# Gate projections in pairs of output tiles: seven products of quarters in place of eight, with the sums on GpSimd

## The chip, the cores and the metric

The kernel runs on one core of one Trainium2 chip. The core has five engines that run side by side: TensorE (PE in the profile, PEld for its weight loads), VectorE (DVE), ScalarE (ACT), GpSimd (POOL) and SyncE (SP, which only starts DMA transfers here). Each takes its instructions in the order of its own queue and waits on semaphores. The metric is the device time of one execution in microseconds (us), lower is better. The kernel before has a median of 964.14 us over 3 runs (963.14 to 965.14).

## The reference

One layer of a mixer trunk in float32: 512 tokens of width 1024 pass a gated mixer of four branches, a cross-attention over 256 memory rows and a gated convolutional feed-forward block, each between RMS norms and with a residual. The part that the change touches is the mixer's gates:

```python
h = rms_norm(x, g[0])                       # (1, 512, 1024)
proj = h @ w_in                             # inputs of the four branches
ya, yb, yc, yd = shortconv(...), gla(...), sgu(...), rglru(...)    # each (1, 512, 256)
y_stack = jnp.stack([ya, yb, yc, yd], axis=2)
branch = jnp.einsum('bskc,kcd->bskd', y_stack, w_branch)           # 4 x 1024 outputs
gates = jax.nn.sigmoid((h @ w_gate).reshape(bsz, s, 4, 1024) + b_gate)   # w_gate: 1024 x 4096
merged = jnp.sum(gates * branch, axis=2)
return merged @ w_mix_out
```

After it follow `x + rms_norm(y)`, the attention, and the feed-forward block with `w_up` (1024 x 5632) and `w_down` (2816 x 1024).

## The kernel before, in words

All activations lie transposed: features on the 128 partitions, the 512 tokens along the free dimension. A projection makes one output tile of 128 features by 512 tokens in one PSUM bank. It runs over eight blocks of 128 input features, and for each block `mm3` (line 124) issues three matmuls, since every float32 operand is split into a high part that the fast float32 format of TensorE holds exactly and a low part that is the rest: high by high, high by low, low by high. So one output tile costs 24 matmuls of 512 columns with a 128x128 weight each.

A weight unit is 128 partitions by 1024 columns, the eight blocks of one output tile side by side (512 KB). `load_unit` (line 69) starts its DMA into a `raw` tile (ring of 4), ScalarE casts it to the high part `whi` (ring of 4, line 75), and VectorE subtracts to get the low part `wlo` (ring of 4, line 76). The list `plan` holds the units in the order of use; `unit` (line 101) loads `LOOK` = 2 units ahead of the one it gives out. A few units near the end (half of `w_o`, one of `w_up`, the last of `w_down`) go through `unit_kept` (line 106), which keeps the split parts in general slots of 512 columns.

The general slots are 76 tiles of 128 x 512 float32, handed out by `get` and returned by `put` (line 54). PSUM's eight banks are three groups: A with 2, B with 4, C with 2 (line 67). The program is written as a straight list of operations. The tile framework adds the semaphores and fixes, when the program is compiled, the order of each engine's queue; operations written earlier have priority, and `tc.high_priority()` raises a few.

Stages in order: load x and the first weights, with token sums of squares on the side (line 242 on); the 18 units of `w_in` (from line 581), between whose blocks `pump` advances the branch fibers (gated linear attention, recurrence, spatial gating), small generators of operations; the gate stage (line 631); the mixer's output projection (`mo`, line 692); keys and values of the memory, which have 256 columns (`kT`, line 729); attention; its output projection; the feed-forward block (`up`, `dn`); the output.

The gate stage runs over the four branches in the order 2, 3, 0, 1, and over eight output tiles each:

```python
    for ki, kb in enumerate(order):
        for m in range(KT):
            if m % 4 == 0:
                wb = unit()
            wg = unit()
            gp = bank("A", "gate")
            dense(gp, wg, xg)
```

`xg` are the eight split blocks of x times the norm's gain; the token's reciprocal norm `rb0s` is multiplied on afterwards, when VectorE drains the bank (`normed`, line 350, recorded at line 352). Then come the branch product of two blocks (six matmuls into a bank of group C), the sigmoid on ScalarE (line 643), gate times branch on VectorE (line 644) and the sum over the branches on VectorE (line 648). In the last branch the sum is split into parts (lines 651 and 152, 153) for the next projection. The original x stays in eight slots through the whole mixer, for the residual (line 707). The last fibers still run when the gate stage begins.

## Time and profile before

| | before |
|---|---|
| median of 3 runs | 964.14 us |
| profiled execution | 964.2 us, span 960.8 us |
| TensorE busy / instructions | 944.7 us (98%) / 4782 matmuls |
| VectorE busy | 575.4 us (60%) |
| ScalarE busy | 420.8 us (44%) |
| GpSimd busy | 11.9 us (1%) |
| DMA | 98.27 MB, mean 102 GB/s |

The span is the time from the first to the last instruction in the profile; the profiled execution's own time has a little around it. Matmuls are pipelined, so that a matmul's duration in the profile is longer than the distance to the next one, and "busy" of TensorE says only that it was not idle. A row of a group gives line, engine, operation, output and inputs, shapes and count, then busy time and mean duration in ns of one, then the engine's idle time just before these instructions with what ended it.

### The profile page before, as it was taken

How to read it: one execution, taken by the hardware profiler on the slowest of the kernel's cores; microseconds unless marked ns; L12 is line 12 of the kernel's file. 1: busy time of each engine (PE TensorE's matmuls, PEld its weight loads, DVE VectorE, ACT ScalarE, POOL GpSimd, SP SyncE). 2: the span in 40 equal slices, each digit the busy share in tenths (PEclk: the TensorE clock that was granted, in tenths of full speed). 3: DMA queues.
4: the chain of work that ended last, by engine and by line, in shares of the span. 5: the costliest groups of instructions: out<-in, count | busy, mean ns of one | idle time of the engine just before them, and what ended most of it. 6: DMA issues, size and time to landing. Idle time of an engine off the chain costs nothing.

```text
span 960.8 us, 12143 instructions
## 1 busy us (share of the span) xinstructions
PE 944.7 (98%) x4782; PEld 801.1 (83%) x4782; DVE 575.4 (60%) x886; ACT 420.8 (44%) x637; POOL 11.9 (1%) x33
## 2 busy tenths in 40 slices
PE   8999999999999999999999999999999999999996
PEld 8878887888888888899888899888888888888885
DVE  5876567535454567359854736887767777522414
ACT  7836336423232534356633645644444444322311
POOL 2000000000000000000000000000000000000001
PEclk9999999999999999999999999999999999999998
DMA  9432121232334332435322420232222323233302
GB/s 333 146 112 88 67 91 63 88 99 78 108 113 148 117 105 67 131 111 190 130 75 66 134 86 2 88 109 88 100 98 89 110 88 98 83 104 99 100 1 87
DMA packets 32648, 98.27 MB, mean 102 GB/s; under 512 B 4288, under 2 KB 7248, under 8 KB 32592
## 3 DMA queue, kind: packets, MB, share of 16 engines
q1 hardware_dynamic: 32416, 97.48, 31.2%
q8 instruction: 37, 0.61, 0.3%
q14 instruction: 19, 0.16, 0.0%
q0 software_dynamic: 32, 0.02, 0.0%
q10 hardware_dynamic: 144, 0.00, 0.0%
HBM read 95.39 MB, written 2.10 MB: 101 GB/s over the span
## 4 chain that ended last, share of the span: by engine, by line
PE 93%; DVE 2%; ACT 2%; issue 2%; DMA 0%; DVEq 0%; ACTq 0%
PE up L127 8%; PE up L126 8%; PE up L125 8%; PE gate L126 6%; PE gate L125 6%; PE gate L127 6%; PE dn L125 4%; PE dn L127 4%; PE dn L126 4%; PE win L125 3%; PE win L127 3%; PE win L126 3%; PE wo L125 2%; PE wo L127 2%; PE wo L126 2%
## 5 line engine op out<-in xcount | busy, mean ns | idle before, releaser
L75 ACT CAST whi<-raw 128x1024 fp32r<-128x1024 f32 x158 | 164.4, 1042 | 301.9 <-issue 142.0
L76 DVE TENSOR_TENSOR wlo<-raw,whi 128x1024 fp32r<-128x1024 f32 x158 | 191.3, 1213 | 130.1 <-ACT whi L75 128.8
L127 PE MATMUL up<-h3h,wlo 128*128 128x512 f32 (+1 forms) x368 | 138.2, 376 | 0.0
L126 PE MATMUL up<-h3l,whi 128*128 128x512 f32 (+1 forms) x368 | 138.1, 375 | 0.0
L125 PE MATMUL up<-h3h,whi 128*128 128x512 f32 (+1 forms) x368 | 138.1, 375 | 0.0
L125 PE MATMUL gate<-xgh,whi 128*128 128x512 f32 x256 | 99.8, 390 | 0.0
L126 PE MATMUL gate<-xgl,whi 128*128 128x512 f32 x256 | 99.7, 389 | 0.0
L127 PE MATMUL gate<-xgh,wlo 128*128 128x512 f32 x256 | 99.6, 389 | 0.0
L125 PEld LDWEIGHTS up<-h3h,whi 128*128 128x128 f32 x368 | 69.3, 188 | 12.6
L126 PEld LDWEIGHTS up<-h3l,whi 128*128 128x128 f32 x368 | 69.3, 188 | 12.4
L127 PEld LDWEIGHTS up<-h3h,wlo 128*128 128x128 f32 x368 | 69.3, 188 | 12.4
L352 DVE TENSOR_TENSOR sg<-gate,rb0s 128x512 f32<-128x512 f32 x32 | 22.1, 691 | 79.0 <-PE gate L127 78.9
L544 DVE SCALAR_TENSOR_TENSOR c<-u,par,c 128x511 f32<-128x511 f32 (+1 forms) x88 | 65.0, 746 | 1.3
L125 PE MATMUL dn<-gh,whi 128*128 128x512 f32 x154 | 59.9, 389 | 0.0
L126 PE MATMUL dn<-gl,whi 128*128 128x512 f32 x154 | 59.9, 389 | 0.0
L127 PE MATMUL dn<-gh,wlo 128*128 128x512 f32 x154 | 59.9, 389 | 0.0
L125 PE MATMUL win<-xgh,whi 128*128 128x512 f32 x144 | 57.1, 397 | 1.8 <-DVE la L535 1.8
L125 PEld LDWEIGHTS gate<-xgh,whi 128*128 128x128 f32 x256 | 48.1, 188 | 10.1
L126 PEld LDWEIGHTS gate<-xgl,whi 128*128 128x128 f32 x256 | 48.1, 188 | 9.9
L127 PE MATMUL win<-xgh,wlo 128*128 128x512 f32 x144 | 56.3, 391 | 0.0
L127 PEld LDWEIGHTS gate<-xgh,wlo 128*128 128x128 f32 x256 | 48.1, 188 | 9.9
L126 PE MATMUL win<-xgl,whi 128*128 128x512 f32 x144 | 56.1, 390 | 0.0
(348 smaller groups left out, 1729.9 us busy)
## 6 DMA issues: line engine op xcount, KB each, us to landing
raw<-in_w_up SPq DMA_DIRECT2D x44, 512.0 KB, 3.5
raw<-in_w_gate SPq DMA_DIRECT2D x32, 512.0 KB, 3.5
raw<-in_w_in SPq DMA_DIRECT2D x18, 512.0 KB, 3.6
raw<-in_w_down SPq DMA_DIRECT2D x16, 512.0 KB, 3.6
raw<-in_w_br SPq DMA_DIRECT2D x8, 512.0 KB, 3.4
raw<-in_w_mix SPq DMA_DIRECT2D x8, 512.0 KB, 3.5
raw<-in_w_k SPq DMA_DIRECT2D x8, 512.0 KB, 3.6
raw<-in_w_v SPq DMA_DIRECT2D x8, 512.0 KB, 3.5
```

Source lines behind the costliest of these rows:

```text
L75: scalar.copy(hi[:, :n], raw[:, :n])
L76: vector.tensor_tensor(lo[:, :n], raw[:, :n], hi[:, :n].bitcast(F32), op=ALU.subtract)
L125: tensor.matmul(ps, lhsT=w[0], rhs=x[0], start=first, stop=False)
L126: tensor.matmul(ps, lhsT=w[0], rhs=x[1], start=False, stop=False)
L127: tensor.matmul(ps, lhsT=w[1], rhs=x[0], start=False, stop=last)
L352: vector.tensor_tensor(t, ps, rb0s, op=ALU.mult)
L544: vector.scalar_tensor_tensor(dst[:, s:S], src[:, 0:S - s], pc(wname, (taps - 1 - s) * stride + off), dst[:, s:S], op0=ALU.mult, op1=ALU.add)
```

## The change

The gate projections take two output tiles at a time. The two weight tiles (256 outputs by 1024 inputs) are cut into quarters: A11 and A12 are the first tile's input blocks 0 to 3 and 4 to 7, A21 and A22 the second's. The input is cut into quarters too: blocks 0 to 3 and 4 to 7, tokens 0 to 255 and 256 to 511 (B11, B12, B21, B22). The four quarters of the result need eight products of quarters; the form of Strassen and Winograd needs seven, with sums of quarters made before and after:

- weights, on GpSimd for each pair: S1 = A21 + A22, S2 = S1 - A11, S3 = A11 - A21, S4 = A12 - S2
- tokens, once, before the later `w_in` units: T1 = B12 - B11, T2 = B22 - T1, T3 = B22 - B12, T4 = B21 - T2, on GpSimd, from copies of x times gain that VectorE makes; each is split into parts again
- products in the order A11 B11, S2 T2, A12 B21, S3 T3, S1 T1, A22 T4, S4 B22, each over four blocks with three matmuls of 256 columns. Three of them add onto an earlier product in the same half bank.

The sums after the products are made when a half bank is drained: one copy on ScalarE, the rest on VectorE, with two multiplications by `rb0s` from SBUF. Weight sums are split into high and low parts as the weights are. A pair makes splits of 1024, 1024, 512 and 1024 columns where two units made two of 1024.

Other edits come with it. The sum over branches is made on GpSimd. The `raw` ring has 5 tiles, `whi` and `wlo` have 6, two tiles `ws` hold the weight sums, the general slots are 70, and the framework's DMA scratch is set smaller. PSUM group A has 3 banks and B has 3. x is given back after the token sums and loaded again after the gate stage. The kept unit of `w_up` and those of `w_down` become ordinary units of the ring. The small load of `walpha` is started by SyncE and not by GpSimd.

```diff
-NSLOT = 76
+NSLOT = 70
+RAW, WHL = 5, 6
...
-        return pp.tile([P, S], F32, tag=tag, bufs={"A": 2, "B": 4, "C": 2}[tag], name=f"{name}_{serial[0]}")
+        return pp.tile([P, S], F32, tag=tag, bufs={"A": 3, "B": 3, "C": 2}[tag], name=f"{name}_{serial[0]}")
+
+    def split_w(src, n):
+        hi = wp.tile([P, 1024], F32R, tag="whi", bufs=WHL, name=f"whi_{serial[0]}")
+        lo = wp.tile([P, 1024], F32R, tag="wlo", bufs=WHL, name=f"wlo_{serial[0]}")
+        serial[0] += 1
+        scalar.copy(hi[:, :n], src)
+        vector.tensor_tensor(lo[:, :n], src, hi[:, :n].bitcast(F32), op=ALU.subtract)
+        return hi, lo
+
+    def load_pair(ap0, ap1):
+
+        raws = []
+        for ap in (ap0, ap1):
+            serial[0] += 1
+            raws.append(wp.tile([P, 1024], F32, tag="raw", bufs=RAW, name=f"raw_{serial[0]}"))
+            sync.dma_start(raws[-1], ap)
+        a11, a12, a21, a22 = [r[:, c:c + S] for r in raws for c in (0, S)]
+        wa, wb = [wp.tile([P, 1024], F32, tag="ws", bufs=2, name=f"ws{i}_{serial[0]}") for i in range(2)]
+        s2, s3, s4, s1 = wa[:, 0:S], wa[:, S:], wb[:, 0:S], wb[:, S:]
+        gpsimd.tensor_add(s1, a21, a22)
+        gpsimd.tensor_sub(s2, s1, a11)
+        gpsimd.tensor_sub(s3, a11, a21)
+        gpsimd.tensor_sub(s4, a12, s2)
+        h0, h1, h3, h2 = split_w(raws[0], 1024), split_w(wa, 1024), split_w(a22, S), split_w(wb, 1024)
+        at = {"a11": (h0, 0), "a12": (h0, S), "s2": (h1, 0), "s3": (h1, S), "a22": (h3, 0), "s4": (h2, 0),
+              "s1": (h2, S)}
...
-        for m in range(KT):
+        for m in range(0, KT, 2):
             plan += [(a["w_br"][kb * 2 + m // 4], 1024)] if m % 4 == 0 else []
-            plan += [(a["w_gate"][kb * KT + m], 1024)]
+            plan += [(a["w_gate"][kb * KT + m], a["w_gate"][kb * KT + m + 1])]
...
-    plan += [(a["w_up"][j], 1024) for j in js[:3]]
+    plan += [(a["w_up"][j], 1024) for j in js]
...
-    for m in range(KT - 1):
+    for m in range(KT):
         plan += [(a["w_down"][m][:, c0 * P:c1 * P], (c1 - c0) * P) for c0, c1 in pieces]
...
-    gpsimd.dma_start(walpha, a["w_alpha"])
+    sync.dma_start(walpha, a["w_alpha"])
...
+    def token_sums():
+
+        out = {n: [] for n in ("b11", "b21", "b22", "t1", "t2", "t3", "t4")}
+        for k in range(KT // 2):
+            x0, x1 = get("xs"), get("xs")
+            vector.tensor_scalar(x0, x[k], gn0[:, k:k + 1], None, op0=ALU.mult)
+            vector.tensor_scalar(x1, x[k + 4], gn0[:, k + 4:k + 5], None, op0=ALU.mult)
+            t12, t34 = get("t12"), get("t34")
+            gpsimd.tensor_sub(t12[:, LO], x0[:, HI], x0[:, LO])
+            gpsimd.tensor_sub(t12[:, HI], x1[:, HI], t12[:, LO])
+            gpsimd.tensor_sub(t34[:, LO], x1[:, HI], x0[:, HI])
+            gpsimd.tensor_sub(t34[:, HI], x1[:, LO], t12[:, HI])
+            put(x0, x1)
+            for names, t in ((("t1", "t2"), t12), (("t3", "t4"), t34)):
+                hi, lo = split(t, "xt", True)
...
+    def seven(wt, xt, name):
+
+        def product(ps, w, xn, more=False):
+            for k in range(4):
+                mm3(ps, wt(w, k), xt[xn][k], k == 0 and not more, k == 3, more)
+                if k % 2:
+                    pump()
+
+        def half():
+            return bank("A", name)[:, 0:256]
+
+        g0, g1, u = get(name), get(name), get("u23")
+        u2, u3 = u[:, LO], u[:, HI]
+        pa = half()
+        product(pa, "a11", "b11")
+        scalar.copy(u2, pa)
+        pb = half()
+        product(pb, "s2", "t2")
+        vector.tensor_tensor(u2, pb, u2, op=ALU.add)
+        product(pa, "a12", "b21", True)
+        vector.tensor_tensor(g0[:, LO], pa, rb0s[:, LO], op=ALU.mult)
+        pc_ = half()
+        product(pc_, "s3", "t3")
+        vector.tensor_tensor(u3, pc_, u2, op=ALU.add)
+        pd = half()
+        product(pd, "s1", "t1")
+        vector.tensor_tensor(g1[:, HI], pd, u3, op=ALU.add)
+        product(pc_, "a22", "t4", True)
+        vector.tensor_tensor(g1[:, LO], pc_, u2, op=ALU.add)
+        product(pd, "s4", "b22", True)
+        vector.tensor_tensor(g0[:, HI], pd, u2, op=ALU.add)
+        vector.tensor_mul(g1, g1, rb0s)
+        vector.tensor_mul(g0[:, HI], g0[:, HI], rb0s[:, HI])
+        put(u)
+        return g0, g1
...
     for p in R2:
         ps = w_in()
         vector.scalar_tensor_tensor(gl_q[p], ps, 0.125, gl_q[p], op0=ALU.mult, op1=ALU.mult)
+    xt = token_sums()
+    put(*x)
     for p in R2:
         rx = normed(w_in(), "rx")
...
-        for m in range(KT):
-            if m % 4 == 0:
+        for m0 in range(0, KT, 2):
+            if m0 % 4 == 0:
                 wb = unit()
-            wg = unit()
-            gp = bank("A", "gate")
-            dense(gp, wg, xg)
+            sgs = seven(unit(), xt, "gate")
             if kb == 1:
                 drain()
-            bp = bank("C", "br")
-            dense(bp, wb, y[kb], base=(m % 4) * 256)
-            sg = normed(gp, "sg")
-            scalar.activation(sg, sg, AF.Sigmoid, bias=pc("bgate", kb * KT + m))
-            vector.tensor_tensor(sg, bp, sg, op=ALU.mult)
-            if ki == 0:
-                acc[m] = sg
-            else:
-                vector.tensor_add(acc[m], acc[m], sg)
-                put(sg)
-                if ki == 3:
-                    merged.append(split(acc[m], "mg", True))
+            for m, sg in zip((m0, m0 + 1), sgs):
+                bp = bank("C", "br")
+                dense(bp, wb, y[kb], base=(m % 4) * 256)
+                scalar.activation(sg, sg, AF.Sigmoid, bias=pc("bgate", kb * KT + m))
+                vector.tensor_tensor(sg, bp, sg, op=ALU.mult)
+                if ki == 0:
+                    acc[m] = sg
+                else:
+                    gpsimd.tensor_add(acc[m], acc[m], sg)
+                    put(sg)
+                    if ki == 3:
+                        merged.append(split(acc[m], "mg", True))
...
+    x = [get(f"x{k}") for k in range(KT)]
+    for k in range(KT):
+        sync.dma_start(x[k], a["xT"][k])
...
-    kept = [unit_kept(a["w_down"][KT - 1][:, c0 * P:c1 * P], (c1 - c0) * P) for c0, c1 in pieces]
+    kept = [unit(0) for _ in pieces]
...
-    nc = _bacc.Bacc("TRN2", target_bir_lowering=False, num_devices=1)
+    nc = _bacc.Bacc("TRN2", target_bir_lowering=False, num_devices=1, dynamic_dma_scratch_size=1024)
```

56 lines of the change are left out of this document (33 added, 23 removed).

## The prediction

> **What bounds the kernel now.** I read the head of the page first, then the chain that ended last, then the stretches and groups of the gate stage, then single instructions.
>
> ```profile
> span 960.8 us, 12143 instructions
> PE 944.7 (98%) x4782; PEld 801.1 (83%) x4782; DVE 575.4 (60%) x886; ACT 420.8 (44%) x637; POOL 11.9 (1%) x33
> PE 93%; DVE 2%; ACT 2%; issue 2%; DMA 0%; DVEq 0%; ACTq 0%
> ```
>
> TensorE (PE) is busy in 98% of the span and holds 93% of the chain. VectorE (DVE) is at 60%, and GpSimd (POOL) is all but unused. The stretches show the same inside the gate stage, which begins near 149 us and ends near 374 us (columns: busy time and instructions of each engine, granted clock, DMA share):
>
> ```profile
> 75.00:149.00 74.00, 74.00 (x387) 61.31 (x386) 45.78 (x69) 33.79 (x42) 1.05 (x2) 1.00 0.26 86
> 149.20:163.00 13.80, 13.24 (x87) 10.60 (x85) 12.62 (x26) 7.70 (x11) 0.00 (x0) 1.00 0.11 39
> 204.21:258.80 54.59, 54.59 (x242) 45.25 (x241) 26.66 (x33) 15.47 (x19) 0.00 (x0) 1.00 0.31 97
> 373.30:418.00 44.70, 44.70 (x201) 37.07 (x200) 22.33 (x31) 21.43 (x31) 0.00 (x0) 1.00 0.33 106
> ```
>
> From 204 to 259 us, one branch's eight output tiles, PE never stops, at full clock (1.00). DVE is busy 26.66 of 54.59 us and ScalarE (ACT) 15.47, so only PE work counts there. At the beginning (149 to 163 us) it is otherwise: the last branch fibers keep DVE busy 12.62 of 13.80 us.
>
> A PE record's duration overlaps the next one's, so the price of a matmul is the distance between starts:
>
> ```profile
> 202.85 0.39 PE L125 MATMUL br<-ych,whi 128*128 128x512 f32 x1
> 209.65 0.39 PE L125 MATMUL br<-ych,whi 128*128 128x512 f32 x1
> 419.04 0.28 PE L126 MATMUL kT<-meml,whi 128*128 128x256 f32 x1
> 420.96 0.28 PE L127 MATMUL kT<-memh,wlo 128*128 128x256 f32 x1
> ```
>
> The first two rows are one output tile apart, 24 gate and 6 branch matmuls: 6.80 / 30 = 0.2267 us for 512 columns. The last two are 16 matmuls apart, each with a new 128x128 weight: 1.92 / 16 = 0.120 us for 256 columns. Half the columns cost 53% of the time. This is the form the change uses.
>
> **The change, part by part.**
>
> *PE.* A pair of output tiles now takes 2 x 8 x 3 = 48 matmuls of 512 columns, 48 x 0.2267 = 10.88 us. Afterwards it takes 7 products x 4 blocks x 3 = 84 of 256 columns, 84 x 0.120 = 10.08 us. The eighth less of arithmetic, 1.36 us, shrinks to 0.80. Sixteen pairs give 12.8 us. The twelve branch matmuls, 2.72 us, stay, so a pair's period on PE goes from 13.60 to 12.80 us. That is the whole possible gain, provided the other engines keep this pace.
>
> *DVE.* The rows that price it:
>
> ```profile
> L76 DVE TENSOR_TENSOR wlo<-raw,whi 128x1024 fp32r<-128x1024 f32 x151 | 184.6, 1225 | 108.3 <-ACT whi L75 107.0
> L352 DVE TENSOR_TENSOR sg<-gate,rb0s 128x512 f32<-128x512 f32 x32 | 22.1, 691 | 79.0 <-PE gate L127 78.9
> L644 DVE TENSOR_TENSOR sg<-br,sg 128x512 f32<-128x512 f32 x32 | 21.9, 685 | 4.0 <-ACT sg L643 4.0
> L648 DVE TENSOR_TENSOR sg<-sg,sg 128x512 f32<-128x512 f32 x24 | 16.6, 690 | 0.7
> L735 DVE TENSOR_TENSOR kl<-kT,kh 128x256 fp32r<-128x256 f32 x8 | 3.3, 417 | 0.3
> L786 DVE TENSOR_SCALAR p<-p,mx 128x256 f32<-128x256 f32 x16 | 4.9, 351 | 0.3
> ```
>
> Per pair before: two and a half weight splits (half a w_br unit), 3.06; normalisation 1.38, product with the branch 1.37, accumulation 1.38: 7.19 us. After: splits of 1024, 1024, 1024 and 512 columns and half a unit, 3 x 1.225 + 0.69 + 0.61 = 4.98; six drains of a half bank at 0.417, 2.50; two normalisations from SBUF, 0.69 + 0.42 = 1.11; the branch products 1.37. That is 9.96 us of 12.80, or 78%. The accumulations go to POOL.
>
> *ACT.*
>
> ```profile
> L75 ACT CAST whi<-raw 128x1024 fp32r<-128x1024 f32 x151 | 158.5, 1051 | 277.7 <-issue 142.0 <-PE win L126 31.1 <-PE dn L126 28.7
> L643 ACT ACTIVATE sg<-sg,par 128x512 f32<-128x512 f32 x32 | 23.0, 719 | 0.0
> L734 ACT CAST kh<-kT 128x256 fp32r<-128x256 f32 x8 | 2.9, 368 | 0.0
> ```
>
> Casts 3 x 1.05 + 0.63 + 0.53, two sigmoids 1.44 and the copy of the first half bank 0.37: 6.1 us of 12.80. Hidden behind PE. If a cast of 1.05 us stood just ahead of that copy, PE would wait 1.05 + 0.37 less the 1.44 us of the product between (12 x 0.120): nothing.
>
> *POOL.* It does four 512-column sums per pair and, from the second branch on, two accumulations. The trace has no such addition, only four of 256 columns at the very end, beside DVE:
>
> ```profile
> 953.49 0.72 POOL L978 TENSOR_TENSOR out<-x,out 128x256 f32<-128x256 f32 x1 [868.68 <-DVE out L976]
> 953.93 0.56 DVE L978 TENSOR_TENSOR out<-x,out 128x256 f32<-128x256 f32 x1
> 954.17 0.91 POOL L978 TENSOR_TENSOR out<-x,out 128x256 f32<-128x256 f32 x1
> 955.41 0.63 DVE L978 TENSOR_TENSOR out<-x,out 128x256 f32<-128x256 f32 x1
> L978 DVE TENSOR_TENSOR out<-x,out x12: 409/416/629, 945.0 to 957.0; 128x256 f32<-128x256 f32 x12
> L976 DVE TENSOR_TENSOR out<-rb,yg x16: 406/414/425, 944.4 to 956.3; 128x256 f32<-128x256 f32 x16
> 1.61 0.29 POOL masks.py:199 TENSOR_SCALAR_AFFINE_SELECT ident<-ident 128x128 f32<-128x128 f32 x1
> 27.94 0.63 POOL L315 TENSOR_SCALAR_AFFINE_SELECT sguw<-sguw 128x512 f32<-128x512 f32 x1 [10.69 <-DMA sguw<-in_sgu_wT]
> ```
>
> The last two rows give POOL's fixed part: 0.34 us for 384 columns leaves 0.18 us. An undisturbed 256-column addition is 0.72, so 0.54 scales, and 512 columns make 0.18 + 1.08 = 1.26 us. Bounds: 0.72 + 0.27, if it grew only as DVE does from 256 to 512 columns (0.417 to 0.69), to 2 x 0.91. I take 1.26, an estimate: 5.0 us per pair in the first branch, 7.6 after, of 12.80.
>
> *POOL against DVE.* The rows show a turn taken. The DVE addition that starts at 953.93, inside a POOL addition, takes 0.56 us, the one at 955.41 0.63, against 0.41 when alone; the POOL addition that follows takes 0.91 against 0.72. DVE's product of a PSUM operand and one SBUF tensor (L976) is not stretched, at most 0.425. So a DVE instruction with two SBUF operands and a POOL addition exclude each other. Not over their whole length: POOL's ended at 954.21, DVE's at 954.49, so 0.28 of its 0.41 us were exclusive. Per pair DVE has 4.98 + 1.11 = 6.09 us of that kind, in 6.5 instructions, some 4.2 exclusive (0.28/0.41); POOL's 7.6 fit beside that, 11.8 of 12.80.
>
> [...]
>
> *What PE waits for.* Three half banks are used twice within a pair. Before its second use DVE or ACT must have drained the first result, in the 1.44 us of the product between. For the third bank (u3) and the fourth (g1, later tokens) the drain is DVE's. It stands in DVE's queue behind any split just started; behind it, in turn, stand the other drains and the splits of the next pair. Best: no stall. Worst: a 1.225 us split held by one POOL addition, then the drain: 1.26 + 1.225 + 0.42 - 1.44 = 1.47 us per pair, 23 us in all. I take 0.2 us, 3.2 in all, near the low end: a weight's slot comes free after the third product of a pair at the earliest (4.3 us), for a weight needed after the twelve branch matmuls (12.8), so splits have some 8 us to go and few must fall into these two windows; nearest row, L352, shows DVE waiting for PE in that place (79.0 us), not PE for DVE.
>
> *The first pair.* Its 9.96 us of DVE work meet a DVE with 13.80 - 12.62 = 1.2 us to spare. Between 0, if the drains go ahead of the fibers, and 8.8 us; I take 2.5, since weight splits of this pair can go earlier, where DVE idles 28 of 74 us.
>
> *Token sums and moves, once.*
>
> ```profile
> L152 ACT CAST mgh<-sg 128x512 fp32r<-128x512 f32 x8 | 5.0, 621 | 13.2 <-DVE sg L648 13.2
> L153 DVE TENSOR_TENSOR mgl<-sg,mgh 128x512 fp32r<-128x512 f32 x8 | 5.5, 692 | 4.7 <-ACT mgh L152 4.7
> L114 ACT CAST kwh<-raw 128x512 fp32r<-128x512 f32 x15 | 9.0, 633 | 4.3 <-DMA raw<-in_w_o 3.5 <-DMA raw<-in_w_up 0.5 <-DMA raw<-in_w_down 0.4
> L115 DVE TENSOR_TENSOR kwl<-raw,kwh 128x512 fp32r<-128x512 f32 x15 | 9.7, 686 | 1.6 <-ACT kwh L114 1.6
> raw<-in_w_mix SPq DMA_DIRECT2D x8, 512.0 KB, 3.5
> ```
>
> Eight scalings on DVE (at most 2 x 0.351 each) and eight splits (0.62 ACT, 0.69 DVE) are 11.1 us of DVE, sixteen POOL subtractions at 0.72 are 11.5 us, all in the 74 us before the gate stage, of which DVE idles 28. With the cover gone they delay the fibers that the first pair waits for: 0 to 3 us, I take 0.5. x is freed and loaded again, eight DMAs of 256 KB in SP's queue among weight loads, at a DMA share of 0.33. They equal four weight loads, 4 x 3.5 = 14 us if one followed the other; the two weights loaded ahead cover 48 x 0.2267 = 10.9. Nothing, or some 3 us if a weight queues behind all eight. Four kept weights become ring units, which saves two halves against a whole on both engines, 4 x (2 x 0.686 + 2 x 0.633 - 1.225 - 1.051) = 1.4 us if nothing hid it; PE shows no idle time there, so nothing. Nor do walpha's DMA, from POOL's queue to SP's, and a bank from group B to A change anything that PE waits for.
>
> *Sum.* The profiled execution took 964.2 us (span 960.8 and 3.4 around it), the median of the three runs is 964.14, so the sum can go against either. 964.2 - 12.8 + 3.2 + 2.5 + 0.5 = 957.6 us. By itself, with the small bounds of its terms: 952 to 962.
>
> **Rivals.**
>
> 1. All of the gain: drains and fibers never late, 964.2 - 12.8 = 951.4 us. For it: the rings' slack; DVE at 78%. Against: DVE at 91% where the stage begins.
>
> 2. No change: DVE and POOL exclude each other for whole instructions. A pair then needs 6.09 + 7.6 = 13.7 us in the last three branches, and PE's 12.80 in the first (6.09 + 5.0 is less). 12 x 13.7 + 4 x 12.80 = 215.6 against 16 x 13.60 = 217.6, that is -2.0, and with 2.5 + 0.5 from above 965.2 us. [...] Against: only 0.28 of 0.41 us exclusive.
>
> 3. Slower: DVE becomes the bound, as it stands idle in its queue while POOL adds. Each of the 6.5 two-SBUF instructions of a pair that waits half a POOL addition, 0.63 us, makes 9.96 + 4.1 = 14.06 us, 0.46 above the old period, in twelve pairs; the first branch has a third less of POOL and stays at PE's pace. 964.2 + 12 x 0.46 - 4 x 0.80 + 2.5 + 0.5 = 969.5 us. It decides from a wait of 0.44 us on (2.84 / 6.5), and loses against before from 0.56. A whole addition at each would end near 1020. For it: waits of 0.15 and 0.22 us in the only two meetings, with additions half as long. Against: the POOL sums come in one burst per pair, and then DVE is free of them.
>
> **How the numbers follow.** Forecast 0.45, rival 1 0.18, rival 2 0.14, rival 3 0.23. Predicted is the forecast's 957.6. Down, the range goes past the full gain with the 1.4 us of the kept weights, to 948. Up, it takes in rival 2 and the nearer half of rival 3, to 976. A measurement of this kernel tells about 0.2% (1.9 us) from no change. Faster by more: the forecast and rival 1, less a sliver, 0.62; within: 0.14; slower: 0.24.
>
> **What would show it.** Right: the 256-column matmuls of the stage start 0.120 us apart; a branch's eight tiles take 51 to 53 us in place of 54.6; PE's idle time in the stage is a few us, put down to DVE drains of half banks and most of it in the first pair; POOL additions of 512 columns take near 1.26 us, longer only beside DVE's two-SBUF instructions. Wrong: starts 0.13 us apart or more, since 0.1295 x 84 = 10.88 eats all of the gain; DVE over 95% busy in the stage; weight splits that wait for POOL and PE waiting for them; POOL additions of 1.6 us and more.

## The result, and the profile after

The changed kernel has a median of 985.72 us (984.65 to 986.06), against 964.21 us of the kernel before on the same chip: a ratio of 1.0222, with a 95% interval of 1.0204 to 1.0239. It is slower, by 21.5 us, where 957.6 had been forecast; the time lies above the whole range. Its profiled execution took 985.39 us.

The head of the changed kernel's page, and the chain that ended last:

```profile
span 983.6 us, 13661 instructions
PE 946.0 (96%) x5358; PEld 825.0 (84%) x5358; DVE 661.2 (67%) x1002; ACT 456.6 (46%) x688; POOL 161.6 (16%) x136
PE 81%; DVE 7%; issue 4%; ACT 3%; POOL 2%; DMA 2%; SPq 0%; DVEq 0%; ACTq 0%; POOLq 0%
```

The span grew by 22.8 us. TensorE holds 81% of the chain in place of 93%, and VectorE 7% in place of 2%. VectorE's 67% alone would not worry anyone: the average hides the stage that counts.

The span splits in three. The gate stage began at 149.4 us before and ended at 374.6, where the first `mo` matmul starts; now it begins at 157.2 and ends at 395.2. The kernel before, in stretches (busy time and instructions of PE, PEld, DVE, ACT, POOL; granted clock, DMA share, GB/s):

```profile
149.40:374.60 225.20, 224.64 (x1026) 185.91 (x1024) 121.05 (x163) 80.56 (x104) 0.00 (x0) 1.00 0.31 101
```

The changed kernel, the same view; the last five rows are short stretches behind stalls:

```profile
157.20:395.20 238.00, 221.41 (x1597) 208.20 (x1596) 189.65 (x263) 107.62 (x145) 120.61 (x78) 0.97 0.31 102
256.00:260.00 4.00, 4.00 (x22) 4.00 (x23) 1.69 (x4) 1.27 (x2) 0.58 (x1) 0.57 0.40 131
285.30:290.00 4.70, 4.70 (x26) 4.60 (x27) 3.08 (x5) 2.34 (x3) 1.28 (x2) 0.66 0.33 112
314.50:319.00 4.50, 4.46 (x31) 4.20 (x32) 3.08 (x6) 2.60 (x3) 1.10 (x2) 1.00 0.31 117
343.00:348.00 5.00, 5.00 (x33) 4.66 (x34) 3.63 (x6) 2.72 (x3) 1.58 (x2) 1.00 0.35 105
369.80:376.00 6.20, 6.20 (x30) 6.20 (x31) 3.48 (x6) 2.28 (x3) 1.92 (x2) 0.53 0.65 218
```

So 7.8 us were lost before the gate stage, 12.8 in it (238.0 against 225.2), and 2.2 behind it (588.4 us from there to the end of the span, against 586.2). Since the matmuls of the stage should have become 12.8 us shorter, the stage lost 25.6 us to something. TensorE is idle for 238.00 - 221.41 = 16.6 us of it, where it had been idle for 0.6: 16.0 more. Three stretches at a clock of 0.57, 0.66 and 0.53 cost, by estimate, (1 - clock) times their length, 1.7 + 1.6 + 2.9 = 6.2 us. Some 3.4 us are left over; the first experiment shows where most of them lie. The idle time is put down to these waits (engine, line, what it waited for: us in all, times, longest):

```profile
PE gate L159 <- DVE u L664: 10.2, 9, 1.8
PE gate L159 <- ACT u L656: 3.5, 2, 3.1
PE gate L159 <- DVE u L659: 2.4, 2, 1.4
```

Line 664 is the drain `u3`, line 659 the drain that makes `u2`, line 656 ScalarE's copy of the first half bank. No wait for a weight is among them. Here is the costliest kind, on the three engines in turn, as single instructions (start, duration; in brackets the idle time before it and what ended it):

```profile
251.42 1.28 POOL L91 TENSOR_TENSOR ws<-raw,ws 128x512 f32<-128x512 f32 x1
...
251.82 1.95 DVE L75 TENSOR_TENSOR wlo<-ws,whi 128x1024 fp32r<-128x1024 f32 x1 [0.62 <-ACT whi L74]
...
252.66 2.24 POOL L745 TENSOR_TENSOR gate<-gate,gate 128x512 f32<-128x512 f32 x1
...
253.69 0.40 PE L160 MATMUL br<-ydl,whi 128*128 128x512 f32 x1
253.70 1.75 DVE L75 TENSOR_TENSOR wlo<-raw,whi 128x512 fp32r<-128x512 f32 x1
...
255.38 0.41 DVE L664 TENSOR_TENSOR u<-gate,u 128x256 f32<-128x256 f32 x1
255.84 0.38 PE L159 MATMUL gate<-xth,whi 128*128 128x256 f32 x1 [1.75 <-DVE u L664]
```

Read it as two engines that pass one thing back and forth. POOL's L91 ends at 251.42 + 1.28 = 252.70. The split that started at 251.82 ends at 253.77, 1.07 us after that; alone it takes 1.22. The POOL addition that started at 252.66 ends at 254.90, 1.13 us after the split; alone it takes 1.28. The next split, 0.68 alone, started at 253.70 and ends at 255.45, 0.55 us after that addition. Each waits for the whole of the other and then runs nearly its full length; only some 0.15 us of its beginning lies beside the other. The drain `u3`, which waits in VectorE's queue behind the two splits, comes at 255.38, and TensorE has stood for 1.75 us.

The longest single wait, 3.08 us before 369.78 in the last branch, comes another way. There GpSimd does a branch sum (line 745) only after two weight sums that stand before it in its queue, and ends it at 368.81. ScalarE's cast of that sum (line 186) waits 4.14 us for it, and the copy of the first half bank (line 656), for which TensorE waits, stands behind the cast in ScalarE's queue. In the whole stage these casts wait:

```profile
ACT mgh L186 <- POOL gate L745: 10.5, 5, 4.1
```

With the low clock behind it (2.9 us) this one stall costs some 6 us.

Line 664 itself isn't stretched. The stage's groups in the changed kernel, by shape (count | busy us, mean ns | idle time before):

```profile
L745 POOL TENSOR_TENSOR gate<-gate,gate 128x512 f32<-128x512 f32 x22 | 32.4, 1485 | 12.0 <-DVE gate L741 12.0
L90 POOL TENSOR_TENSOR ws<-raw,raw 128x512 f32<-128x512 f32 x14 | 26.3, 1876 | 0.0
...
L109 DVE TENSOR_TENSOR wlo<-raw,whi 128x1024 fp32r<-128x1024 f32 x11 | 21.1, 1914 | 1.4 <-ACT whi L108 1.4
...
L75 DVE TENSOR_TENSOR wlo<-raw,whi 128x512 fp32r<-128x512 f32 x15 | 15.6, 1038 | 0.9 <-ACT whi L74 0.9
...
L664 DVE TENSOR_TENSOR u<-gate,u 128x256 f32<-128x256 f32 x16 | 6.6, 413 | 0.0
```

The 1914 ns of line 109 are a mixture: the seven `w_br` splits take 2.29 to 2.31 us each, and four splits of the next projection, at the end of the stage, 1.22 to 1.23. Splits of 512 columns take 1038 ns in the mean, POOL's additions up to 1876. The drains, with one operand in PSUM, keep their 413 ns.

### The profile page after: what moved, and what is told of

It is laid out like the page before. It is cut to its first block, busy times and chain, and to the rows that moved or that the text cites. A ratio compares the mean times of both kernels' runs of the same rounds, so it can differ in the third digit from the quotient of the medians.

```text
span 983.6 us, 13661 instructions
## 1 busy us (share of the span) xinstructions
PE 946.0 (96%) x5358; PEld 825.0 (84%) x5358; DVE 661.2 (67%) x1002; ACT 456.6 (46%) x688; POOL 161.6 (16%) x136
## 4 chain that ended last, share of the span: by engine, by line
PE 81%; DVE 7%; issue 4%; ACT 3%; POOL 2%; DMA 2%; SPq 0%; DVEq 0%; ACTq 0%; POOLq 0%
PE up L160 8%; PE up L161 8%; PE up L159 8%; PE dn L159 4%; PE dn L161 4%; PE dn L160 4%; PE gate L159 4%; PE gate L160 4%; PE gate L161 4%; PE win L159 3%; PE win L160 3%; PE win L161 3%; DVE wlo L75 2%; PE wo L159 2%; PE wo L161 2%
## 5 line engine op out<-in xcount | busy, mean ns | idle before, releaser
L109 DVE TENSOR_TENSOR wlo<-raw,whi 128x1024 fp32r<-128x1024 f32 (+1 forms) x130 | 164.9, 1273 | 126.2 <-ACT whi L108 124.6
L108 ACT CAST whi<-raw 128x1024 fp32r<-128x1024 f32 (+1 forms) x130 | 134.3, 1037 | 175.9 <-PE dn L160 62.8
L159 PE MATMUL gate<-xth,whi 128*128 128x256 f32 x256 | 75.2, 294 | 12.6 <-DVE u L664 10.2
L161 PE MATMUL gate<-xth,wlo 128*128 128x256 f32 x256 | 73.6, 287 | 0.0
L160 PE MATMUL gate<-xtl,whi 128*128 128x256 f32 x256 | 73.5, 287 | 0.0
L161 PE MATMUL dn<-gh,wlo 128*128 128x512 f32 (+1 forms) x198 | 72.6, 367 | 0.0
L159 PE MATMUL dn<-gh,whi 128*128 128x512 f32 (+1 forms) x198 | 72.5, 366 | 0.0
L160 PE MATMUL dn<-gl,whi 128*128 128x512 f32 (+1 forms) x198 | 72.4, 366 | 0.0
L159 PEld LDWEIGHTS gate<-xth,whi 128*128 128x128 f32 x256 | 50.1, 196 | 16.8 <-DVE u L664 14.0
L159 PE MATMUL gate<-xgh,whi 128*128 128x256 f32 x192 | 56.3, 293 | 3.6 <-ACT u L656 3.5
```

Source lines behind the costliest of these rows:

```text
L108: scalar.copy(hi[:, :n], raw[:, :n])
L109: vector.tensor_tensor(lo[:, :n], raw[:, :n], hi[:, :n].bitcast(F32), op=ALU.subtract)
L159: tensor.matmul(ps, lhsT=w[0], rhs=x[0], start=first, stop=False, skip_group_check=more)
L160: tensor.matmul(ps, lhsT=w[0], rhs=x[1], start=False, stop=False, skip_group_check=more)
L161: tensor.matmul(ps, lhsT=w[1], rhs=x[0], start=False, stop=last, skip_group_check=more)
```

## The experiments

**Theory and rivals after the result.** Theory A: a POOL addition and a VectorE instruction with two SBUF operands exclude each other from end to end, so VectorE stands in its queue with the drains behind it, and that is what TensorE waits for. Theory B: VectorE simply has too much to do, or it is the order of the seven products. Theory C: the smaller rings and the other buffers. Beside these, the token sums were suspected of the 7.8 us at the beginning.

### GpSimd out of the gate stage

```diff
-        wa, wb = [wp.tile([P, 1024], F32, tag="ws", bufs=2, name=f"ws{i}_{serial[0]}") for i in range(2)]
-        s2, s3, s4, s1 = wa[:, 0:S], wa[:, S:], wb[:, 0:S], wb[:, S:]
-        gpsimd.tensor_add(s1, a21, a22)
-        gpsimd.tensor_sub(s2, s1, a11)
-        gpsimd.tensor_sub(s3, a11, a21)
-        gpsimd.tensor_sub(s4, a12, s2)
+        wa, wb = raws[1], raws[0]
...
-                    gpsimd.tensor_add(acc[m], acc[m], sg)
+                    vector.tensor_add(acc[m], acc[m], sg)
```

The weight sums are left out here: the products take raw quarters in their place, so the gates are not those of the reference. Splits, products, drains and token sums all stay.

> The changed kernel with GpSimd taken out of the gate stage: the four weight sums are left out (the raw quarters are split in their place, as many splits of the same size), and the sum over the branches is made on VectorE again. The products are then not those of the gates. Theory (VectorE's two-operand instructions and GpSimd's additions shut each other out, and that makes the drains late): TensorE's idle time in the stage falls under 6 us, splits are back at 1.22 us, the stage takes 215 to 223 us, the total is 963 to 971. Rival (VectorE is simply too full, and one product too short a time for a drain, whatever GpSimd does): idle time stays over 10 us, stage over 230, total over 977.

Measured: 960.05 us, ratio 0.9967 (0.9954 to 0.998). The gate stage as one stretch, then the only wait of PE in it, then two groups:

```profile
157.20:372.40 215.20, 214.00 (x1599) 202.56 (x1598) 175.99 (x287) 108.37 (x145) 0.00 (x0) 1.00 0.35 114
```

```profile
PE gate L154 <- DVE u L654: 1.0, 1, 1.0
```

```profile
L104 DVE TENSOR_TENSOR wlo<-raw,whi 128x1024 fp32r<-128x1024 f32 x11 | 13.4, 1220 | 1.4 <-ACT whi L103 1.4
...
L75 DVE TENSOR_TENSOR wlo<-raw,whi 128x512 fp32r<-128x512 f32 x15 | 10.3, 684 | 0.0
```

All of these splits are back at 1220 and 684 ns, where 2.31 us and 1038 ns stood. VectorE has more instructions than in the changed kernel (287 against 263), since the branch sums are its own again, and is busy for less time (175.99 against 189.65 us). The stage takes 215.2 us: 22.8 less than with POOL at work, and 10.0 less than before. So GpSimd's work in the stage cost 22.8 us. Theory A explains the splits and the drains behind them; the run also takes away the late branch sums of the last branch, and does not separate the two. Of theory B the part that says "too much to do" falls, at least for this amount of work.

By the prediction's sum the stage should take 225.2 - 12.8 = 212.4 us, and 2.8 us of the gain are still missing here, without any work on GpSimd. TensorE is idle for 1.2 us, and the pairs are 12.9 and 13.0 us apart in place of 12.80 (ScalarE's copies, line 651, start at 256.98, 269.86 and 282.86). So most of the 3.4 us that were left over above are no matter of late drains.

### The branch sums alone back on VectorE

```diff
-                    gpsimd.tensor_add(acc[m], acc[m], sg)
+                    vector.tensor_add(acc[m], acc[m], sg)
```

> The changed kernel with one edit: the sum over the branches is made on VectorE again; GpSimd keeps the weight sums. Theory (time in which GpSimd holds the shared operands): 24 of 88 additions, some 31 of 138 us of GpSimd's, are gone from the stage; TensorE's idle time falls from 16 to 6 to 11 us, the stage takes 224 to 232 us in place of 238, total 972 to 980 us. Rival (only the weight sums, which come in one burst per pair, meet the splits, and VectorE gets 17 us more to do): stage 236 us or more, total 983 or more.

Measured: 974.15 us, ratio 1.0102 (1.008 to 1.0124). The gate stage:

```profile
157.20:385.20 228.00, 217.98 (x1596) 204.17 (x1595) 201.75 (x286) 107.34 (x145) 88.17 (x56) 0.99 0.33 108
```

The stage is some 10 us shorter than the changed kernel's although VectorE does the additions now (the stretches of these runs begin up to 0.2 us off the first gate matmul). From 238.0 to 228.0 us here, and from there to the 215.2 of the run above: taken away in this order, the branch sums on POOL cost some 10 us, the weight sums on POOL another 13. In the first part is the stall of some 6 us in the last branch: the wait at line 656 falls from 3.5 to 0.5 us.

### Half as long, twice as many

Weight sums of 256 columns in place of 512, twice as many: if it is the longest single hold that matters, this helps; if the total time held, it harms.

```diff
-        gpsimd.tensor_add(s1, a21, a22)
-        gpsimd.tensor_sub(s2, s1, a11)
-        gpsimd.tensor_sub(s3, a11, a21)
-        gpsimd.tensor_sub(s4, a12, s2)
+        for q in (slice(0, 256), slice(256, S)):
+            gpsimd.tensor_add(s1[:, q], a21[:, q], a22[:, q])
+            gpsimd.tensor_sub(s2[:, q], s1[:, q], a11[:, q])
+            gpsimd.tensor_sub(s3[:, q], a11[:, q], a21[:, q])
+            gpsimd.tensor_sub(s4[:, q], a12[:, q], s2[:, q])
```

> The changed kernel with one edit: each weight sum on GpSimd is made in two instructions of 256 columns. Theory A (the length of one hold counts, since a drain waits behind a split that waits for one addition): a split waits at most 0.7 us in place of 1.3, TensorE's idle time falls to 8 to 12 us, total 975 to 981 us. Theory B (the whole time held counts): GpSimd needs 2 x 0.72 in place of 1.30 us per sum, 9 us more in all; idle time stays at 15 to 19 us, total 983 to 990.

Measured: 989.68 us, ratio 1.027 (1.0247 to 1.0293), slower than the change by some 4 us more. Two groups of POOL, then PE's largest waits:

```profile
L92 POOL TENSOR_TENSOR ws<-raw,ws 128x256 f32<-128x256 f32 x28 | 37.8, 1352 | 0.0
...
L90 POOL TENSOR_TENSOR ws<-ws,raw 128x256 f32<-128x256 f32 x28 | 20.7, 740 | 57.3 <-issue 57.3
```

```profile
PE gate L160 <- DVE u L665: 14.7, 9, 2.3
```

A half takes 740 ns where it runs nearly free (line 90), more than half of 1.28 us, and 1352 where it has to wait (line 92). Shorter turns only mean more of them, and TensorE's wait at the drain `u3` (line 665 here) grows from 10.2 to 14.7 us.

### All sums on VectorE

```diff
-        gpsimd.tensor_add(s1, a21, a22)
-        gpsimd.tensor_sub(s2, s1, a11)
-        gpsimd.tensor_sub(s3, a11, a21)
-        gpsimd.tensor_sub(s4, a12, s2)
+        vector.tensor_add(s1, a21, a22)
+        vector.tensor_sub(s2, s1, a11)
+        vector.tensor_sub(s3, a11, a21)
+        vector.tensor_sub(s4, a12, s2)
...
-                    gpsimd.tensor_add(acc[m], acc[m], sg)
+                    vector.tensor_add(acc[m], acc[m], sg)
```

> The changed kernel with the weight sums and the sum over the branches on VectorE, none on GpSimd in the gate stage. Theory (VectorE's own work is the bound then): 9.96 + 4 x 0.69 + 2 x 0.69 = 14.1 us per pair by durations, over TensorE's 12.8; the stage takes 224 us or more, total 969 to 978. Rival (what counts is the distance between starts, 0.60 for 0.69 us: 12.4 us per pair): it fits, stage 215 to 220 us, total 960 to 966.

Measured: 975.47 us, ratio 1.0123 (1.0104 to 1.0142). The stage, and PE's one kind of wait in it:

```profile
157.30:386.20 228.90, 215.85 (x1596) 203.00 (x1596) 203.56 (x339) 105.04 (x140) 0.00 (x0) 0.99 0.33 106
```

```profile
PE gate L159 <- DVE u L659: 13.0, 11, 2.9
```

VectorE is busy for 203.56 of 228.9 us and TensorE waits for its drains again, with nothing on POOL. So the sums have no cheap place: on POOL they take VectorE's time by holding it up, on VectorE they take it by their own length. With the branch sums on VectorE either way, the two places cost the same: 228.9 us here, 228.0 with the weight sums on POOL.

### The order of the products

The third product, which adds onto the first half bank, goes behind `S3 T3`, so that the copy of the first half bank and the drain `u3` of the third have the time of two products and not of one.

```diff
+        pc_ = half()
+        product(pc_, "s3", "t3")
+        vector.tensor_tensor(u3, pc_, u2, op=ALU.add)
         product(pa, "a12", "b21", True)
         vector.tensor_tensor(g0[:, LO], pa, rb0s[:, LO], op=ALU.mult)
-        pc_ = half()
-        product(pc_, "s3", "t3")
-        vector.tensor_tensor(u3, pc_, u2, op=ALU.add)
```

> The changed kernel with one edit: the products run in the order A11 B11, S2 T2, S3 T3, A12 B21, S1 T1, A22 T4, S4 B22, so that the first and third half banks are drained in the time of two products (2.87 us) and not one (1.44 us). Theory (late drains): TensorE's idle time in the gate stage, 16.1 us put down to u3 (10.2), the copy u2 (3.5) and the addition to u2 (2.4), falls under 5 us, the clock dips of the stage (0.94 to 0.98) go with it, the stage takes 218 to 224 us in place of 238, and the total is 965 to 972 us. [...]

Measured: 974.94 us, ratio 1.0119 (1.0104 to 1.0134). That is some 11 us better than the change, and short of what was expected: the stage takes 228.1 us, where 218 to 224 had been forecast. The two largest waits of PE in the stage:

```profile
PE gate L159 <- DVE gate L667: 4.9, 5, 1.2
PE gate L159 <- DVE u L659: 4.1, 3, 2.0
```

The wait at `u3` (line 664, 10.2 us) is gone, and 4.9 us of it have turned up at the next half bank with a short interval, line 667. With 2.4 us at line 656 the three come to 11.4 us, after 16.1. The order of the products matters about as much as the branch sums on POOL, but much of the wait only moves.

### The token sums later

Token sums behind the branch fibers' last `w_in` unit. So that the framework could not bring the scalings forward, they take their gain from a copy `gnl` that depends on a late value and equals `gn0`.

```diff
-            vector.tensor_scalar(x0, x[k], gn0[:, k:k + 1], None, op0=ALU.mult)
-            vector.tensor_scalar(x1, x[k + 4], gn0[:, k + 4:k + 5], None, op0=ALU.mult)
+            vector.tensor_scalar(x0, x[k], gnl[:, k:k + 1], None, op0=ALU.mult)
+            vector.tensor_scalar(x1, x[k + 4], gnl[:, k + 4:k + 5], None, op0=ALU.mult)
...
-    xt = token_sums()
-    put(*x)
...
+    gnl = cp.tile([P, KT], F32, name="gnl")
+    vector.scalar_tensor_tensor(gnl, sc[0][:, 0:KT], 0.0, gn0, op0=ALU.mult, op1=ALU.add)
+    xt = token_sums()
+    put(*x)
```

> The changed kernel with one edit: the token sums are written after the two ac projections and are made to wait for them, so that they can't be moved to the beginning of the program. Theory (the token sums stand in VectorE's and ScalarE's queues ahead of the branch fibers' first steps): the first gate matmul starts near 151 us in place of 157.2, total 978 to 981 us. Rival (the larger rings do it: more splits of w_in units go ahead of the fibers): the first gate matmul stays at 156 to 158 us, total 984 to 988.

Measured: 981.78 us, ratio 1.0184 (1.0169 to 1.0199), nearly 4 us better than the change and just outside the 978 to 981 expected. The first gate matmul comes at 151.8 us in place of 157.2, and the stage is as long as the changed kernel's, 237.9 us. The profiled execution, the fastest of the four with 979.74 us, so keeps the whole 5.4 us. The stage still begins 4.3 us later than with the buffers alone (147.5, next section); TensorE waits for other things of the fibers, 1.9 us among them for `ktt`.

The cause lies further forward than where the token sums are written. The changed kernel's opening: an instruction of VectorE, two stretches, and a wait of PE.

```profile
12.18 0.49 DVE L622 TENSOR_SCALAR xs<-x,gn 128x512 f32<-128x512 f32 x1
```

```profile
0.00:75.00 75.00, 68.04 (x396) 58.54 (x396) 62.61 (x126) 54.48 (x100) 20.72 (x40) 1.00 0.55 190
75.00:85.00 10.00, 7.10 (x24) 5.77 (x25) 5.11 (x7) 4.58 (x6) 0.00 (x0) 0.83 0.59 202
```

```profile
PE gr L591 <- issue: 3.6, 1, 3.6
```

The framework brought the token scalings up to 12.18 us, into the loading of x, ahead of work that TensorE needs. The next section has the same stretches without token sums.

### The buffers alone

The kernel before with nothing but the changed kernel's buffers and moves: `raw` 5, `whi` and `wlo` 6, 70 slots, PSUM 3, 3 and 2, the kept units in the ring, the smaller DMA scratch, `walpha` on SyncE. Gates in eight products as before. The core of the diff against the kernel before:

```diff
-NSLOT = 76
+NSLOT = 70
+RAW, WHL = 5, 6
...
-        return pp.tile([P, S], F32, tag=tag, bufs={"A": 2, "B": 4, "C": 2}[tag], name=f"{name}_{serial[0]}")
+        return pp.tile([P, S], F32, tag=tag, bufs={"A": 3, "B": 3, "C": 2}[tag], name=f"{name}_{serial[0]}")
...
-    gpsimd.dma_start(walpha, a["w_alpha"])
+    sync.dma_start(walpha, a["w_alpha"])
...
-    kept = [unit_kept(a["w_down"][KT - 1][:, c0 * P:c1 * P], (c1 - c0) * P) for c0, c1 in pieces]
+    kept = [unit(0) for _ in pieces]
```

> The kernel before with the changed kernel's buffers alone: rings of 5 raw and 6 split tiles, 70 slots, bank groups of 3, 3 and 2, the w_up and w_down units in the ring, the smaller DMA scratch, walpha on SyncE's queue. Gates stay eight dense products, no token sums, x kept. Theory (token sums cost the 7.8 us before the gate stage): 963 to 966 us. Rival (rings): 968 to 973 us, with the first gate matmul at 153 to 157 us in place of 149.4.

Measured: 961.52 us, ratio 0.9988 (0.9979 to 0.9998). Theory C falls: the buffers cost nothing, they gain a little. The stretches that stand against those above:

```profile
0.00:75.00 75.00, 70.60 (x414) 61.88 (x415) 54.94 (x117) 53.41 (x97) 5.56 (x24) 1.00 0.60 210
75.00:85.00 10.00, 10.00 (x45) 8.28 (x45) 10.00 (x13) 6.42 (x8) 0.00 (x0) 1.00 0.32 107
147.50:372.70 225.20, 224.70 (x1026) 185.86 (x1024) 120.91 (x163) 80.60 (x103) 0.00 (x0) 1.00 0.30 101
```

With the same buffers and no token sums the gate stage begins at 147.5 us, 9.7 us before the changed kernel's. By 75 us the changed kernel is behind by 414 - 396 = 18 matmuls, and in the next ten by another 21: there TensorE stands for 3.6 us at the recurrence's small matmuls, and the mean clock is 0.83. If all were of 512 columns, at 0.2267 us each, 39 matmuls are 8.8 us. That is most of the 9.7 us, lost before the first weight of the gates is loaded (98.2 us). With the token sums written later, in the section before this one, the two stretches hold 414 and 45 matmuls, as with the buffers alone; so it is the token sums that cost the opening its some 9 us. For the wait at line 591 itself the profile names no releaser. 1.9 us of the 9.7 were hidden in the comparison with the kernel before, because the buffers win as much. A wait of the kernel before in the opening, which isn't there with the new buffers, is of that size:

```profile
PE win L125 <- DVE la L535: 1.8, 1, 1.8
```

### Seven products in three branches only

Next a version that avoids each of the costs: the first branch keeps eight products, the token sums go into that branch, where VectorE has room, the branch sums are VectorE's, the products are in the new order.

```diff
-                plan += [(a["w_gate"][kb * KT + m], a["w_gate"][kb * KT + m + 1])]
+            if ki < 1:
+                plan += [(a["w_gate"][kb * KT + m + i], 1024) for i in range(2)]
+            else:
+                plan += [(a["w_gate"][kb * KT + m], a["w_gate"][kb * KT + m + 1])]
...
-            sgs = seven(unit(), xt, "gate")
+            if ki >= 1:
+                sgs = seven(unit(), xt, "gate")
...
+                if ki < 1:
+                    gp = bank("A", "gate")
+                    dense(gp, unit(), xg)
...
+                    if m == 1:
+                        gnl = cp.tile([P, KT], F32, name="gnl")
+                        vector.scalar_tensor_tensor(gnl, sg[:, 0:KT], 0.0, gn0, op0=ALU.mult, op1=ALU.add)
+                        xt = token_sums(gnl)
+                        put(*x)
...
-                    gpsimd.tensor_add(acc[m], acc[m], sg)
+                    vector.tensor_add(acc[m], acc[m], sg)
```

> Seven products in the last three branches only; the first branch keeps eight dense tiles, and the token sums are made in it, after its second tile. The products run in the order of the first experiment, and the sum over the branches is on VectorE. Theory: the 10 us that the token sums cost ahead of the gate stage (157.2 against 147.2 us for the first gate matmul with these buffers and no token sums) are gone, since VectorE has half of its time free in that branch; twelve pairs save 12 x 0.80 = 9.6 us of TensorE time, less what the weight sums on GpSimd still hold up (0.3 to 0.8 us per pair): 955 to 962 us. Rival (the token sums cost as much wherever they stand, or the sums on GpSimd eat the whole 0.80): 964 us or more.

Measured: 973.75 us, ratio 1.01 (1.0083 to 1.0116), far above the 955 to 962 expected. The stage begins at 149.2 us, as hoped, but TensorE waits once for long:

```profile
PE br L162 <- DVE sg L747: 8.4, 1, 8.4
```

All token sums in one place put one long wait of 8.4 us in front of a drain. Then they were spread, one block after each of the tiles 1 to 4 and its splits two tiles later:

```diff
-                    if m == 1:
-                        gnl = cp.tile([P, KT], F32, name="gnl")
+                    if 1 <= m < 1 + 4:
+                        gnl = tp.tile([P, KT], F32, tag="gnl", bufs=4, name=f"gnl{m}")
                         vector.scalar_tensor_tensor(gnl, sg[:, 0:KT], 0.0, gn0, op0=ALU.mult, op1=ALU.add)
-                        xt = token_sums(gnl)
-                        put(*x)
+                        token_sums(m - 1, gnl)
+                    if 3 <= m < 3 + 4:
+                        token_splits(m - 3)
```

> As the experiment with seven products in the last three branches (order of products changed, branch sums on VectorE), with the token sums spread over the first branch: for one pair of input blocks after each of the tiles 1 to 4, their splits after the tiles 3 to 6. Theory (in that experiment VectorE and ScalarE stood still 8.4 us behind the token sums of GpSimd, as all four blocks were written in one place): this stall and the clock dip behind it go, 12 pairs at 13.3 us and a first branch of 54.6, the stage takes 215 to 220 us in place of 236, total 953 to 959 us. Rival (GpSimd's additions hold up the tiles around them wherever they stand): the stage over 226, total 963 or more.

Measured: 962.10 us, ratio 0.9984 (0.9972 to 0.9997), above the 953 to 959 expected, with the first gate matmul at 147.3 us and the stage at some 224. The long wait is gone and the beginning is clean, but the gain expected of twelve pairs did not come. What PE waited for:

```profile
PE gate L162 <- DVE u L666: 4.5, 5, 1.8
```

The instructions, with ScalarE's copy of the first half bank (line 663) as the mark of each pair:

```profile
303.38 0.37 ACT L663 COPY u<-gate 128x256 f32<-128x256 f32 x1 [0.91 <-PE gate L164]
...
316.26 0.37 ACT L663 COPY u<-gate 128x256 f32<-128x256 f32 x1 [0.61 <-PE gate L164]
...
317.99 1.75 POOL L91 TENSOR_TENSOR ws<-raw,ws 128x512 f32<-128x512 f32 x1
318.50 2.31 DVE L75 TENSOR_TENSOR wlo<-raw,whi 128x1024 fp32r<-128x1024 f32 x1
320.73 0.41 DVE L666 TENSOR_TENSOR u<-gate,u 128x256 f32<-128x256 f32 x1
...
330.03 0.37 ACT L663 COPY u<-gate 128x256 f32<-128x256 f32 x1 [0.90 <-PE gate L164]
...
343.96 0.37 ACT L663 COPY u<-gate 128x256 f32<-128x256 f32 x1 [0.61 <-PE gate L164]
...
360.60 0.35 ACT L663 COPY u<-gate 128x256 f32<-128x256 f32 x1
```

The distances are 12.9 and 13.8 and, in the last branch, 13.9 and 16.6 us. In every second pair a split starts inside a POOL addition (318.50 against 317.99 to 319.74), takes 2.31 in place of 1.22 us, and has the drain `u2` (320.73) behind it. Eight products take 13.60. So half of the pairs earn 0.7 us, the others give 0.2 back and one in the last branch 3.0. In that one two splits of finished branch sums stand before the drain as well: it comes at 349.61, TensorE has stood for 1.83 us, and from 348 to 356 us the mean granted clock is 0.79. The stage comes to some 224 us against the 225.2 of eight products.

Whether the half microsecond per pair could be had by putting each split behind the drain in VectorE's queue by hand was not tried.

The same with the branch sums on POOL, to see their price once more in the mended kernel:

```diff
-                    vector.tensor_add(acc[m], acc[m], sg)
+                    gpsimd.tensor_add(acc[m], acc[m], sg)
```

> The kernel with the spread token sums, but with the sum over the branches on GpSimd as in the change. Theory (held time): 24 more additions of 1.3 us beside the splits; TensorE waits 0.3 to 0.8 us more per pair than in the kernel with them on VectorE, total 4 to 10 us above it, and in the last branch the casts of the sums wait for GpSimd. Rival (with the longer windows for the drains it makes no difference, and VectorE gets 17 us less to do): within 2 us of it, or faster.

Measured: 965.67 us, ratio 1.0022 (1.0011 to 1.0032), 3.6 us above the other, a little less than the 4 to 10 expected. And the buffers alone once more, beside these two:

> The kernel before with the changed kernel's buffers alone, once more, beside the two kernels above. It gave 0.9988 of before; the same is expected, 961 to 963 us, and that the kernel with seven products in three branches stands 3 to 8 us below it if its theory holds.

Measured: 960.90 us, ratio 0.9969 (0.9957 to 0.9981). It stands 1.2 us below the version with seven products in three branches, which should have been 3 to 8 us faster; the runs of the two overlap (959.78 to 962.10 and 960.82 to 964.56). What that version wins against the kernel before is what the buffers win; seven products in place of eight bring nothing in this kernel, in the best form that was found. The kernel with the lowest median that does the whole computation is the old one with the new buffers.

## Why the prediction was wrong

**TensorE's part was nearly right.** The 256-column matmuls start 0.120 us apart in the stage, and with POOL out of the way it takes 215.2 us where the sum's 225.2 - 12.8 is 212.4. Some 10 us of the 12.8 showed there.

**The step that failed is the term for late drains: "I take 0.2 us" per pair, 3.2 in all.** With the first pair's 2.5 us the sum held 5.7 us for drains that come late. In their place the gate stage lost 25.6 us: TensorE stood idle for 16.0 us more than before, 6.2 went with the clock behind the stalls, and 3.4 are left, of which the run without POOL's work shows most as well. Taking that work away won back 22.8 us. The first pair is not where it happened: TensorE's waits in the first 13 us of the stage sum to 1.9 us, near the 2.5 taken, while the prediction expected most of the idle time there. The worst case of the prediction, 1.47 us a pair and 23 us in all, was built as the trace has it, a split held by an addition with the drain behind it, and the four longest such waits are 1.75 to 1.77 us. The reason given for the low end was that splits have some 8 us to go in and few fall into the two windows. That treats the windows as a matter of chance. But the queue's order is fixed when the program is compiled, and the same order comes back: the stall of 255.84 is there again at 285.29, 314.54 and 342.98, every four output tiles. The path through ScalarE, a cast that waits for a branch sum on POOL with the copy behind it, was not in the sum at all; it is some 6 of the 25.6 us.

**Behind the low term stands an exclusion read from the right rows with the wrong arithmetic.** The prediction found that "0.28 of its 0.41 us were exclusive" and used that as a share: 4.2 of 6.09 us per pair. The 0.13 us that overlap are a fixed piece at the beginning of an instruction, not a third of it. The splits of the changed kernel show 1.07 of 1.22 us and 0.55 of 0.68 exclusive, thus about 0.15 overlapping at either length. By that, 6.09 us in 6.5 instructions are some 5.1 exclusive, and with 7.6 of POOL 12.7 of 12.80 in place of 11.8: no slack, though by itself it would still have fitted. One instruction length was measured, and a constant and a proportion look the same in one row.

**The rivals.** The second came nearest to the mechanism: it took exclusion over the whole length, where the splits show 1.07 of 1.22 us and 0.55 of 0.68. It was too kind with it: it packed the two engines perfectly, 965.2 us. The third had the consequence, VectorE standing in its queue, and its far end: "a whole addition at each would end near 1020". The time lies between the two ends of the third. What all of them left out is that the wait needs no engine to be full: VectorE is busy for 189.65 of 238 us in the stage, its waits inside held instructions included. It was a drain's lateness that counted, not the sum of a pair's work.

**The token sums: 0.5 us taken, some 9 measured.** The bounds were 0 to 3. The prediction put them in the 74 us before the gate stage, by the place where they are written. They ran from 12.18 us on, in the opening, where VectorE was busy for 54.94 of 75 us without them, and with them came the wait of 3.6 us at line 591 and the low clock beside it (0.83 from 75 to 85 us), which the run with late token sums does not have.

**The rest.** POOL's 512-column addition, estimated at 1.26 us, takes 1.28 to 1.30 alone. The sum had no term for weights that come late, and no wait of TensorE for a weight appears. It took the buffers at nothing, and they bring 0.1 to 0.3%. The 2.2 us behind the stage were not in the sum, though the bound of some 3 us for x, loaded again, would cover them. With the buffers alone that part takes 958.7 (the span) - 372.7 = 586.0 us, no more than before; what is left there of the change is x, loaded again. That this is the cause was argued only.

## What to carry to other kernels

Before giving GpSimd work that reads SBUF, add up its time and that of VectorE's instructions with two SBUF operands: if both together come near the period, expect them to cost TensorE time, as here (6.09 and 7.6 us beside a period of 12.80, and 22.8 us of the stage), whatever the busy shares say. Price a late drain by what can stand in front of it in the queue, not by the mean load; where the order is fixed at compile time, one bad place can be paid turn after turn, as the 1.75 to 1.77 us were four times here. And when work is added early in a program that a scheduler orders, look where it lands in the trace and not where it is written.

## What the runs showed of the hardware

**Stalls and the clock.** In the changed kernel's stage four stalls of TensorE last 1.75 to 1.77 us, and behind two of them (255.84 above, and 285.29 us) the granted clock is 0.57 and 0.66 over the next 4 to 5 us; behind the other two (314.54 and 342.98) it is 1.00. Behind the one of 3.08 us (369.78) it is 0.53 for 6 us. PE's first matmuls behind them, with the idle time in brackets:

```profile
285.29 0.39 PE L159 MATMUL gate<-xth,whi 128*128 128x256 f32 x1 [1.76 <-DVE u L664]
...
314.54 0.38 PE L159 MATMUL gate<-xth,whi 128*128 128x256 f32 x1 [1.75 <-DVE u L664]
...
342.98 0.39 PE L159 MATMUL gate<-xth,whi 128*128 128x256 f32 x1 [1.77 <-DVE u L664]
...
369.78 0.58 PE L159 MATMUL gate<-xgh,whi 128*128 128x256 f32 x1 [3.08 <-ACT u L656]
```

So, with the estimate above, a stall can cost nearly twice its length (1.75 us and another 1.7 at 255.84, 3.08 and another 2.9 at 369.78), and equal stalls cost differently: 1.75 us of standing had a low clock behind them at 255.84 and none at 314.54. What decides between the two was not shown.

**GpSimd's fixed cost.** A 256-column half of a weight sum takes 740 ns free, a 512-column one 1.28 to 1.30 us, so a fixed part of some 0.2 us by estimate (2 x 0.74 - 1.29); cutting its work into shorter turns made the kernel some 4 us slower still.
